# Moving one subtraction of the sliding-window attention from GpSimd to VectorE in a one-core trunk kernel

## The chip, the cores and the metric

The kernel runs on one core of one Trainium2 chip. The metric is the device time of one execution, in microseconds (us); less is better. A core has five engines that work at the same time, each through its own list of instructions in a fixed order: TensorE (PE in the profile, with its weight loads as PEld), VectorE (DVE), ScalarE (ACT), GpSimd (POOL) and SyncE (SP), which here only issues DMAs. An instruction that has to wait for another engine holds up everything behind it in its own list.

## The reference

One decoder layer is computed for a prompt of 2048 tokens (plus 16 meta tokens in front) and for a group of 8 x 4 sample tokens. Each token passes a normalisation, a wide input projection, three groups of heads side by side (HGRN2, mLSTM, and attention over a sliding window of 128 keys with a sink), an output projection and a SwiGLU feed-forward layer. The change touches the attention of the prompt, whose core is

```python
s = einsum('bnqhgd,bnshd->bnhgqs', q, k) * HD_C ** -0.5
s = where(mask, s, NEG_BIG)
mx = maximum(max(s, axis=-1), sink)
p = exp(s - mx)
den = sum(p, axis=-1) + exp(sink - mx)
o = einsum('bnhgqs,bnshd->bqnhgd', p / den, v)
```

There are 8 query heads in two groups (the variable `kv`) of four, 64 wide, and each block of 128 queries sees its own 128 keys and the 128 before them.

## The kernel before

The arithmetic is meant to be close to single precision, while TensorE is fed 16-bit operands. So an operand is split into a high part (rounded to float16) and a low part (the difference between the value and its high part, again in float16), and a product is made of three matmuls: high x high, high x low, low x high.

The prompt is worked through in tiles of 128 tokens. For each tile `project` makes the input projections in pieces of the weight matrix (named `qf`, `bqk`, `cq`, `ckv`, `aig` and `bvo`), all through the helper at L212, and then `mix` runs three generators side by side: `swa_prompt` (attention), `mlstm_prompt` and `hgrn_prompt`. After the mixer, from about 842 us on in the profiled execution, come the output projection, the preparation of the feed-forward operands and the feed-forward layer itself. One tile of the mixer takes about 46 us.

The order in which an engine's list is written is not the order of the source: the framework schedules the instructions with a timing model of its own when the program is built, so moving an instruction to another engine also changes the order of others around it. On the chip the lists are fixed, and engines wait for one another by semaphores.

In `swa_prompt` the steps for each tile are these. The scores of a head pair come from TensorE (L810) and are masked and reduced on VectorE (L813). ScalarE takes the exponentials and their sums (L819). VectorE makes the reciprocal of the denominators, `sden` (L824). Then, for each of the two groups `kv`:

- GpSimd multiplies the four heads' weights, 128 x 256 each, by the reciprocal (L834), in place in `pb`;
- ScalarE writes the high part `hi`, 128 x 1024, into the tile `ph` (L835);
- SyncE issues a DMA that transposes `hi` into `pT` (L836);
- GpSimd subtracts, `lo = pb - hi`, 128 x 1024, into the second half of `ph` (L837);
- SyncE issues the transposing DMA of `lo` (L838).

At the end TensorE multiplies the transposed weights with the values (L845, the tile `oc`), and ScalarE and VectorE write the result (L854, L855). `ph` has one buffer, so the high part of the second group (L835) can't be written before both transposes of the first group have read `ph`. `pT` has two buffers.

Beside it on VectorE run the HGRN2 levels (L540, L549, L551, each level feeding the next level's matmuls at L527), with their decay products `t` on GpSimd (L553); the mLSTM gates (L622 to L636, among them a series of tiny 128 x 4 instructions at L634), its row statistics (L648 to L676, which feed the matmul at L678) and its masked scores (L689, L698); and the low parts of the projections (L325, L350, L353), which wait for the high parts from ScalarE and are waited for by DMAs at L326 and L351.

Of the kernel before, what the change touches and what calls it, by code (L numbers as in the profile page):

```python
# [14 lines left out]
ALU = mybir.AluOpType  # L15
# [44 lines left out]
def trunk(ctx, tc, I, O, groups):  # L60
    nc = tc.nc
    V, S, G, T = nc.vector, nc.scalar, nc.gpsimd, nc.tensor
# [15 lines left out]
    def pmt(name="m"):  # L78
        return pm.tile([P, 512], F32, tag="m", name=nm(name))
# [42 lines left out]
    def zt(tag, shape, dt=F32, bufs=1):  # L122
        return pz.tile(shape, dt, tag=tag, bufs=bufs, name=nm(tag))
# [365 lines left out]
    def small(tag, cols=8):  # L489
        return am_(tag, [P, cols], bufs=2)  # L490
# [300 lines left out]
    def swa_prompt(s, yT, off):  # L791
        L = s.L
        prev = carry["kv"]
        blocks = ([prev] if prev else []) + [(s.kx, s.cvx)]
        nbk = len(blocks)
        W = nbk * P
        mask = (swm if s.chunk >= 2 else swm1).rearrange("p a k -> p (a k)")[:L, 2 * P - W :]
        mx = small("mx", 8)[:L]
        den = small("sden", 8)[:L]
        pms = []  # L800
        for kv in range(2):
            pb = zt(f"pb{kv}", [P, 4, 2 * P])
            pms.append(pb)
            for gp in range(2):
                ps = pmt("ss")
                for u in range(2):
                    g = 2 * gp + u
                    for o, (kx, _) in enumerate(blocks):
                        for a in range(2):
                            T.matmul(ps[:L, u * 256 + o * P : u * 256 + o * P + P], s.qx[kv][:, g], kx[:, kv, a], start=(a == 0), stop=(a == 1))  # L810
                for u in range(2):
                    hd = kv * 4 + 2 * gp + u
                    V.tensor_tensor_reduce(pb[:L, 2 * gp + u, :W], ps[:L, u * 256 : u * 256 + W], mask, 0.125 / (QS * QS), -3.0e38, ALU.add, ALU.max, mx[:, hd : hd + 1])  # L813
                yield
        ng = small("ng", 8)[:L]
        V.scalar_tensor_tensor(ng, mx, -1.0, nsink[:L], op0=ALU.mult, op1=ALU.min)
        for hd in range(8):
            pb = pms[hd // 4][:L, hd % 4, :W]
            S.activation(pb, pb, AF.Exp, bias=ng[:, hd : hd + 1], accum_out=den[:, hd : hd + 1])  # L819
        es = small("es", 8)[:L]  # L820
        V.tensor_tensor(es, ng, sink[:L], op=ALU.add)
        S.activation(es, es, AF.Exp)
        V.tensor_tensor(den, den, es, op=ALU.add)
        V.reciprocal(den, den)  # L824
        pts = []
        for kv in range(2):

            ph = zt("ph", [P, 2, 4, 2 * P], F16)
            pt = zt("pT", [P, 2, 8, P], F16, bufs=2)[:, :, : 4 * nbk, :L]
            pts.append(pt.rearrange("p a (g b) t -> p a b g t", b=nbk))  # L830
            hi, lo = (ph[:L, a].rearrange("p g k -> p (g k)")[:, : 4 * W] for a in range(2))
            pb = pms[kv][:L, :, :W]
            for g in range(4):
                G.tensor_scalar(pb[:, g], pb[:, g], den[:, kv * 4 + g : kv * 4 + g + 1], PS, op0=ALU.mult, op1=ALU.mult)  # L834
            S.activation(hi.rearrange("p (g k) -> p g k", g=4), pb, AF.Copy)  # L835
            nc.sync.dma_start(pt[:, 0], hi, transpose=True)  # L836
            G.tensor_tensor(lo.rearrange("p (g k) -> p g k", g=4), pb, hi.rearrange("p (g k) -> p g k", g=4), op=ALU.subtract)  # L837
            nc.sync.dma_start(pt[:, 1], lo, transpose=True)  # L838
            yield
        po = pmt("oc")  # L840
        order = [(b, p, r) for b in range(nbk) for p, r in ((0, 0), (1, 0), (0, 1))]
        for b, p, r in order:
            for kv in range(2):
                o_ = slice(kv * 64, kv * 64 + 64)
                T.matmul(po[o_, : 4 * L].rearrange("p (g t) -> p g t", g=4), blocks[b][1][:, p, o_], pts[kv][:, r, b], start=(b, p, r) == order[0], stop=(b, p, r) == order[-1])  # L845
        pv = po[:, : 4 * L].rearrange("p (g t) -> p g t", g=4)
        put_yT(yT, 4, pv, off, L, YS / (PS * VS))
        carry["kv"] = (s.kx, s.cvx)
        yield

    def put_yT(yT, j0, pv, off, L, scale=YS):
        hi = yT[:, 0, j0 : j0 + 4, off : off + L]
        lo = yT[:, 1, j0 : j0 + 4, off : off + L]
        S.activation(hi, pv, AF.Copy, scale=scale)  # L854
        V.scalar_tensor_tensor(lo, pv, scale, hi, op0=ALU.mult, op1=ALU.subtract)  # L855

    def mixer_prompt(s, yT, off):
        y = zt("y", [P, 512])
        interleave(swa_prompt(s, yT, off), mlstm_prompt(s, y[:, 256:512]), hgrn_prompt(s, y[:, 0:256]))
        finish_y(y, yT, off, s.L)  # L860
# [348 lines left out]
    with (  # L1209
# [136 lines left out]
        for gi, grp in enumerate(groups):  # L1346
# [35 lines left out]
            for rw in sum(rows2, []):  # L1382
# [9 lines left out]
                if t == 0:  # L1392
                    k = min(L, NS - r0)
# [313 lines left out]
```

## Time and profile before

| what | before |
|---|---|
| median of 3 runs | 2424.07 us (2414.37 to 2427.03) |
| the profiled execution | 2414.44 us |
| span of its instructions | 2412.7 us |
| busy: TensorE / VectorE / ScalarE / GpSimd | 92% / 70% / 39% / 50% of the span |
| mean granted TensorE clock | 0.970 |
| L837 on GpSimd | 34 instructions, the first at 91.7 us and the last at 837.9 us |

The last row says where the change acts: in the first 842 us, which hold all the mixer tiles of the prompt. The page's list of the chain that ended last names only the final additions and stores, a few us in all, so it says nothing about this stage; the stage has to be read from its windows, its waits and its order of time. In the rows that follow, "a <- b" behind an instruction is the tile that it writes and those that it reads, and a bracket at the end tells how long the engine was idle before the instruction and what ended that.

### The profile page before, as it was taken

Reading aid. Unit: us, or ns where it says so; the run is one execution under the profiler, and the core shown is the slowest. Engines: PE = TensorE matmul, PEld = TensorE weight load, DVE = VectorE, ACT = ScalarE, POOL = GpSimd, SP = SyncE. Lnnn points to the kernel's source line nnn. Section 1 sums busy time; section 2 is a strip of 40 time slices with the busy share of each in tenths; the row PEclk is TensorE's granted clock in tenths of the full one; section 3 lists DMA queues with packets and bytes.
Section 4 is the critical chain, followed back from the end, with each engine's and each line's share of the span. In section 5 each row is a group of like instructions: output and inputs, shape, how many; then the busy total and the mean of one; then the engine's idle time right before and its main releaser. Section 6 shows DMA issues by size and latency. Waiting matters only on the chain. (4 is left out here: it accounts for less than half of the span.)

```text
span 2412.7 us, 51978 instructions
## 1 busy us (share of the span) xinstructions
PE 2220.3 (92%) x20298; PEld 1607.4 (67%) x20298; DVE 1679.2 (70%) x4030; ACT 943.5 (39%) x2526; POOL 1211.7 (50%) x1629
## 2 busy tenths in 40 slices
PE   6989999999999899896989979889999999999996
PEld 6677767767776445444657556567686767888886
DVE  8788988988988756558879677746454535655546
ACT  7554455554554432334343434422212123332323
POOL 7344344444443464549778788744232324544435
PEclk9999999999999899997999989899999999999998
DMA  7232333333223755996436545684324247744441
GB/s 258 50 63 69 66 67 68 75 61 74 66 64 73 173 183 192 275 330 222 153 139 231 196 158 191 191 287 185 148 108 168 108 152 199 269 176 175 177 174 38
DMA packets 294329, 364.95 MB, mean 151 GB/s; under 512 B 203808, under 2 KB 234480, under 8 KB 294067
## 3 DMA queue, kind: packets, MB, share of 16 engines
q1 hardware_dynamic: 285090, 331.02, 43.6%
q0 software_dynamic: 4384, 15.93, 1.7%
q10 hardware_dynamic: 4608, 14.68, 1.7%
q8 instruction: 159, 2.61, 0.4%
q14 instruction: 88, 0.71, 0.1%
HBM read 212.24 MB, written 103.50 MB: 131 GB/s over the span
## 5 line engine op out<-in xcount | busy, mean ns | idle before, releaser
L1239 PE MATMUL s<-x,w 128*128 128x384 f16 (+1 forms) x5544 | 826.4, 312 | 14.8 <-DMA w<-wgu_scratch 6.2
L1239 PEld LDWEIGHTS <-w 128*128 128x128 f16 x5544 | 542.6, 98 | 296.5 <-issue 13.8
L1292 PE MATMUL dn<-w,hh 128*128 128x256 f16 (+1 forms) x4158 | 444.4, 278 | 56.0 <-ACT hh L1268 23.6
L1292 PEld LDWEIGHTS <-hh 128*128 128x128 f16 (+1 forms) x4158 | 379.6, 99 | 119.8 <-ACT hh L1268 27.8
L212 PEld LDWEIGHTS <-xT 128*128 128x128 f16 (+1 forms) x1992 | 177.4, 99 | 191.4 <-issue 25.2
L1268 ACT ACTIVATE hh<-tmp 128x384 f16<-128x384 f32 (+1 forms) x231 | 112.4, 494 | 280.4 <-DVE tmp L1262 164.5
L1248 POOL TENSOR_TENSOR tmp<-tmp,tmp 128x384 f32<-128x384 f32 (+1 forms) x66 | 65.3, 990 | 279.0 <-ACT tmp L1247 271.8
L1269 DVE TENSOR_TENSOR hh<-tmp,hh 128x384 f16<-128x384 f32 (+1 forms) x231 | 144.5, 633 | 74.2 <-ACT hh L1268 72.5
L212 PE MATMUL wo<-wo,xT 128*128 128x512 f16 x768 | 180.8, 394 | 9.5 <-DVE xn L992 4.6
L156 DVE SCALAR_TENSOR_TENSOR w<-raw,w 128x512 f16<-128x512 f32 (+1 forms) x136 | 111.9, 855 | 7.0 <-ACT w L155 6.9
L1250 DVE TENSOR_TENSOR tmp<-s,tmp 128x384 f32<-128x384 f32 (+1 forms) x66 | 34.2, 518 | 107.3 <-PE s L1239 107.3
L212 PE MATMUL d<-xT,qf 128*128 128x128 f16 (+1 forms) x1632 | 107.7, 220 | 0.0
L156 DVE SCALAR_TENSOR_TENSOR w<-sums,w 128x1024 f16<-128x1024 f32 x68 | 96.9, 1427 | 11.4 <-ACT w L155 11.4
L1259 ACT ACTIVATE tmp<-tmp 128x384 f32<-128x384 f32 (+1 forms) x132 | 61.6, 489 | 107.9 <-DVE tmp L1250 52.6
L212 PE MATMUL d<-xT,bqk 128*128 128x128 f16 (+1 forms) x1632 | 100.6, 221 | 3.2 <-DVE e L278 3.2
L1324 DVE SCALAR_TENSOR_TENSOR xr<-dn,xr 128x256 f32<-128x256 f32 x192 | 78.7, 417 | 34.4 <-PE dn L1292 30.2
L212 PEld LDWEIGHTS <-qf 128*128 128x128 f16 x1632 | 94.4, 100 | 9.1 <-issue 4.1
L212 PEld LDWEIGHTS <-bqk 128*128 128x128 f16 x1632 | 94.0, 100 | 5.4 <-issue 4.5
L212 PE MATMUL d<-xT,cq 128*128 128x128 f16 (+1 forms) x1632 | 96.2, 217 | 0.0
L212 PE MATMUL d<-bvo,xT 128*128 128x512 f16 (+1 forms) x408 | 96.2, 380 | 0.0
L1262 DVE SCALAR_TENSOR_TENSOR tmp<-tmp,tmp 128x384 f32<-128x384 f32 (+1 forms) x132 | 71.9, 558 | 34.1 <-POOL tmp L1249 32.6
L212 PE MATMUL d<-aig,xT 128*128 128x512 f16 (+1 forms) x408 | 92.4, 379 | 3.4 <-DVE g L358 3.4
(536 smaller groups left out, 4064.6 us busy)
## 6 DMA issues: line engine op xcount, KB each, us to landing
w<-wgu_scratch SPq DMA_DIRECT2D x88, 896.0 KB
wgu_scratch<-w SPq DMA_DIRECT2D x44, 896.0 KB
w<-wdn_scratch SPq DMA_DIRECT2D x44, 896.0 KB
raw<-in_w_ffn_in_dram SPq DMA_DIRECT2D x88, 256.0 KB
wdn_scratch<-w SPq DMA_DIRECT2D x22, 896.0 KB
xs<-in_x_prompt_dram SPq DMA_DIRECT2D x26, 512.0 KB
x_scratch<-pT ACTq DMA_DIRECT2D x28, 448.0 KB
raw<-in_w_ffn_out_dram SPq DMA_DIRECT2D x22, 512.0 KB
```

The costliest lines, as they stand in the source:

```text
L156: V.scalar_tensor_tensor(lo, src, scale, hi, op0=ALU.mult, op1=ALU.subtract)
L212: T.matmul(out, lh(k, a), rh(k, b), start=(n == 0), stop=(n == 3 * nk - 1))
L1239: T.matmul(out, A[k // 2][p][:, a, k % 2 * P : k % 2 * P + P], x2[r][:, k // 2, op, k % 2, :n], start=i == 0, stop=i == 11)
L1248: G.tensor_tensor(r12, r12, r22, op=ALU.add)
L1250: V.tensor_tensor(r11, prod(A12, B21), r11, op=ALU.add)
L1259: S.activation(d, d, AF.Silu, scale=UF)
L1262: V.scalar_tensor_tensor(d, v, UF * HS, d, op0=ALU.mult, op1=ALU.mult)
L1268: S.activation(hi, v, AF.Copy)
L1269: V.tensor_tensor(lo, v, hi, op=ALU.subtract)
L1292: T.matmul(out, hh[p][:, q, a, off : off + L], ws[q][r][:, b], start=(q, p, r) == order[0], stop=(q, p, r) == order[-1])
L1324: V.scalar_tensor_tensor(x[:L, cc], m, UD, x[:L, cc], op0=ALU.mult, op1=ALU.add)
```

## The change

One word of one line: the subtraction that makes the low part of the attention weights is issued on VectorE (`V`) and no longer on GpSimd (`G`). Operands, shapes, types and buffers stay as they are.

```diff
             S.activation(hi.rearrange("p (g k) -> p g k", g=4), pb, AF.Copy)
             nc.sync.dma_start(pt[:, 0], hi, transpose=True)
-            G.tensor_tensor(lo.rearrange("p (g k) -> p g k", g=4), pb, hi.rearrange("p (g k) -> p g k", g=4), op=ALU.subtract)
+            V.tensor_tensor(lo.rearrange("p (g k) -> p g k", g=4), pb, hi.rearrange("p (g k) -> p g k", g=4), op=ALU.subtract)
             nc.sync.dma_start(pt[:, 1], lo, transpose=True)
```

Thirty-four instructions move, two for each of the 17 mixer tiles (32 of 128 x 1024, two of 16 x 512 for the meta tokens). Since the scheduler runs again, other instructions move with them: up to about the middle of the program on the engines' lists the order differs, and the feed-forward layer behind it is in the same order as before.

GpSimd's list in one middle tile, as a difference (`-` stands in the kernel before only). `ph_8520` and `ph_8558` are the first and the second group's `ph`, `t_...` are the decay products of the HGRN2 levels.

```order
 L834 TENSOR_SCALAR pb_1047_8427<-pb_1047_8427,sden_8355 128x256 x4
 L553 TENSOR_TENSOR t_1077_8584<-t_1072_8556 128x8
-L837 TENSOR_TENSOR ph_8520<-pb_1036_8356,ph_8520 128x1024
 L553 TENSOR_TENSOR t_1082_8619<-t_1077_8584 128x2x2
 L373 TENSOR_TENSOR ga_9150<-ga_9150,gA_448 128x256
-L837 TENSOR_TENSOR ph_8558<-pb_1047_8427,ph_8558 128x1024
 L553 TENSOR_TENSOR t_1087_8639<-t_1082_8619 128x2
```

Both subtractions leave the list; the four multiplications of the second group (the first row shown) stand ahead of them before and after.

VectorE's list in the same tile, at the place where they come in.

```order
+L837 TENSOR_TENSOR ph_8520<-pb_1036_8356,ph_8520 128x1024
+L350 SCALAR_TENSOR_TENSOR kx_9109<-d_9060,kx_9109 64x128
 L540 COPY_PREDICATED att_8377<-lv_45_381,lv_8574 64x4x2x16 x2
 L549 TENSOR_TENSOR qz_465<-qz_465,t_1072_8556 64x2x4x16 x2
 L551 TENSOR_TENSOR k_8017<-k_8017,t_1072_8556 128x8x16
-L325 SCALAR_TENSOR_TENSOR qlo_9053<-d_8954,qx_1123_9052 64x512
-L350 SCALAR_TENSOR_TENSOR kx_9109<-d_9060,kx_9109 64x128 x2
+L350 SCALAR_TENSOR_TENSOR kx_9109<-d_9060,kx_9109 64x128
 L353 SCALAR_TENSOR_TENSOR cvx_9110<-d_9060,cvx_9110 128x128
 L358 SCALAR_TENSOR_TENSOR g_9119<-d_9060,gbias_454 128x8
 L622 SCALAR_TENSOR_TENSOR ax_9269<-g_9119 128x4
+L837 TENSOR_TENSOR ph_8558<-pb_1047_8427,ph_8558 128x1024
```

The two subtractions stand ten instructions apart in the new list, and one HGRN2 level and the low parts of the keys and values lie between them. Of the first fifteen full tiles this is the one with the least work between the two; in the sixteenth and last only four small copies stand between them.

SyncE's list in the same tile, which holds the DMAs of `ph`.

```order
+L326 DMA qx_1122_9051<-qlo_9053 64x512
 L836 DMA_TRANSPOSE pT_8521<-ph_8520 128x8x128
-L326 DMA qx_1122_9051<-qlo_9053 64x512
 L326 DMA qx_1123_9052<-qlo_9053 64x512
+L838 DMA_TRANSPOSE pT_8521<-ph_8520 128x8x128
 L351 DMA kx_9109<-kx_9109 64x256 x2
-L838 DMA_TRANSPOSE pT_8521<-ph_8520 128x8x128
 L836 DMA_TRANSPOSE pT_8559<-ph_8558 128x8x128
```

The transpose of the first low part (L838 of `pT_8521`) now stands ahead of the two copies of the keys (L351) and no longer behind them.

## The prediction

> **What bounds the kernel now.** I read the windows first, cut where the mixer tiles begin and end. Columns: length, then busy time and (x) instructions of PE, PEld, DVE, ACT and POOL, the granted clock, and the DMA share and rate.
>
> ```profile
> 0.00:120.00 120.00, 99.76 (x1362) 77.91 (x1363) 96.49 (x329) 74.52 (x211) 65.55 (x109) 0.97 0.48 154
> 120.00:842.00 722.00, 664.98 (x8009) 509.26 (x8006) 624.74 (x1985) 362.24 (x1206) 306.16 (x545) 0.99 0.34 77
> 842.00:2412.70 1570.70, 1455.52 (x10932) 1020.21 (x10932) 957.97 (x1717) 506.75 (x1111) 839.94 (x976) 0.96 0.53 185
> ```
>
> The subtraction lies in the first two rows. In the second TensorE is busy 665.0 of 722 us (92%) and VectorE 624.7 (87%); GpSimd, which gives the work up, is at 42%. So TensorE leaves 57.0 us idle there, and this is all that any edit of the other engines can win in that stage. Next I read what TensorE waits for (total us, times, longest):
>
> ```profile
> PE lv L527 <- DVE k L551: 24.6, 21, 3.8
> PE Mb L678 <- DVE mb L676: 20.4, 12, 4.7
> PE oc L845 <- DMA pT<-ph: 6.4, 8, 1.6
> ```
>
> 45 of the 57 us are waits for VectorE (HGRN2 levels, mLSTM row statistics). Only 6.4 us are waits for the transposed weights that the subtraction helps to make. So VectorE is second in line, and work added to it can surface on TensorE; GpSimd stands in none of these rows.
>
> **What goes away.** The costliest group of GpSimd in this stage:
>
> ```profile
> L837 POOL TENSOR_TENSOR ph<-pb,ph 128x1024 f16<-128x1024 f32 x32 | 68.9, 2154 | 25.0 <-ACT ph L835 25.0
> ```
>
> With two small ones this is 71 us of GpSimd time, which by itself is worth nothing, since nobody on TensorE waits for GpSimd. But the order of time shows a second cost. Start, duration, instruction; the first and the last of 23 cases, one in between, and the next tiny VectorE instruction behind that one:
>
> ```profile
> 134.56 2.16 POOL L837 TENSOR_TENSOR ph<-pb,ph 128x1024 f16<-128x1024 f32 x1 [3.29 <-ACT ph L835]
> 134.76 2.11 DVE L549 TENSOR_TENSOR qz<-qz,t 64x128 f32<-64x128 f32 x1
> 545.91 2.13 POOL L837 TENSOR_TENSOR ph<-pb,ph 128x1024 f16<-128x1024 f32 x1 [0.83 <-ACT ph L835]
> 545.95 2.12 DVE L634 SCALAR_TENSOR_TENSOR pp<-pp,z 128x4 f32<-128x4 f32 x1
> 548.32 0.15 DVE L635 SCALAR_TENSOR_TENSOR pp<-pp,z 128x4 f32<-128x4 f32 x1
> 837.85 2.20 POOL L837 TENSOR_TENSOR ph<-pb,ph 128x1024 f16<-128x1024 f32 x1 [4.38 <-ACT ph L835]
> 837.79 2.41 DVE L549 TENSOR_TENSOR qz<-qz,t 64x128 f32<-64x128 f32 x2
> ```
>
> A 128 x 4 instruction that takes 0.15 us takes 2.12 us when it meets the subtraction: VectorE stands still until GpSimd is done, although the profile counts it as busy. Taking from each VectorE instruction that overlaps an L837 the usual time of its own kind (the tenth percentile), 23 of the 34 subtractions stretch one by more than 0.1 us, together **39.7 us**. So the true cost of the subtraction to VectorE is already 39.7 us.
>
> **What is added.** No row has this subtraction on VectorE. The nearest rows (count, then minimum/median/maximum in ns) are one of the same width and types with one more operand, and one of the same operation and types with 384 elements:
>
> ```profile
> L205 DVE SCALAR_TENSOR_TENSOR xn<-xs,ss,xn x15: 1270/1280/1286, 34.3 to 655.2; 128x1024 f16<-128x1024 f32 x15
> L1269 DVE TENSOR_TENSOR hh<-tmp,hh x231: 432/551/1348, 1087.7 to 2368.0; 128x384 f16<-128x384 f32 x77, 128x280 f16<-128x280 f32 x39
> ```
>
> I take the first, 1.28 us: 32 x 1.28 = 41.0, and 1.3 for the two small ones: **42.3 us**. The low end scales the second up at one element per ns: 0.55 + 0.64 = 1.19 us, or 39.4 in all. The Trainium skill, "GPSIMD Engine Reference", section "Performance versus the Vector engine", gives a two-input elementwise operation as 1.96 times slower on GpSimd; by that factor the 2.15 us of the row above would be an estimated 1.10 us, the term 36 us and the result 2 us lower. Against the stretch that goes, the busy time of VectorE changes by 42.3 - 39.7 = +2.6 us: next to nothing.
>
> **A new wait.** The subtraction of the second group needs its high part, and that needs `ph` free of the first group's transposes. On GpSimd this wait harmed nobody; on VectorE everything behind it waits too (in the changed order the mLSTM gates and scores and the next HGRN2 level). The chain in one tile: first subtraction, its DMA on SyncE, second high part.
>
> ```profile
> 538.90 2.12 POOL L837 TENSOR_TENSOR ph<-pb,ph 128x1024 f16<-128x1024 f32 x1
> 541.55 1.31 SPq L838 DMA_TRANSPOSE pT<-ph  x1
> 544.78 1.06 ACT L835 ACTIVATE ph<-pb 128x1024 f16<-128x1024 f32 x1 [1.95 <-DMA pT<-ph]
> ```
>
> From the issue of the DMA to the high part are 3.23 us, then 1.06 us of writing it: 4.3 us at least from the end of the first subtraction to the start of the second, 4.9 with the 0.5 us that the DMA stood behind other issues here. What VectorE has to do meanwhile is in the changed order; its durations, for the tile with the least:
>
> ```profile
> 539.43 0.28 DVE L350 SCALAR_TENSOR_TENSOR kx<-d,kx 64x128 f16<-64x128 f32 x1
> 540.05 0.29 DVE L350 SCALAR_TENSOR_TENSOR kx<-d,kx 64x128 f16<-64x128 f32 x1 [0.34 <-ACT kx L349]
> 540.69 0.29 DVE L353 SCALAR_TENSOR_TENSOR cvx<-d,cvx 128x128 f16<-128x128 f32 x1 [0.34 <-ACT cvx L352]
> 540.90 0.15 DVE L358 SCALAR_TENSOR_TENSOR g<-d,gbias 128x8 f32<-128x8 f32 x1
> 541.09 0.16 DVE L622 SCALAR_TENSOR_TENSOR ax<-g 128x4 f32<-128x4 f32 x1
> 542.02 0.60 DVE L540 COPY_PREDICATED att<-lv,lv 64x128 f32<-64x128 int32 x2
> 542.66 0.59 DVE L549 TENSOR_TENSOR qz<-qz,t 64x128 f32<-64x128 f32 x2
> 543.26 0.29 DVE L551 TENSOR_TENSOR k<-k,t 128x128 f32<-128x128 f32 x1
> ```
>
> These add up to 2.65 us, with some 0.7 of waits for ScalarE (brackets). Done in the same way for all 16 full tiles the work between is 0.9 (the last tile) to 6.8 us, 4.1 on average. Against 4.3 us, with those waits counted as cover, VectorE would stand 5 us in all; against 4.9 and without them 15. I take **10 us**. The first subtraction waits for less:
>
> ```profile
> 534.65 0.20 DVE L824 RECIPROCAL sden<-sden 128x8 f32<-128x8 f32 x1
> 536.93 1.06 ACT L835 ACTIVATE ph<-pb 128x1024 f16<-128x1024 f32 x1 [0.16 <-POOL pb L834]
> ```
>
> That is 3.3 us from the reciprocal to the high part, and mostly over 3.6 us of VectorE work lie there in the changed order: nothing, in the first tiles up to 1 us each, within the bounds above.
>
> **A collision that stays.** The first subtraction will run while GpSimd multiplies the second group's weights. What that does is seen a little earlier in the same tile, against the same pair undisturbed (0.59 us, above):
>
> ```profile
> 535.02 3.75 POOL L834 TENSOR_SCALAR pb<-pb,sden 128x256 f32<-128x256 f32 x8 [2.50 <-DVE sden L824]
> 536.16 0.87 DVE L549 TENSOR_TENSOR qz<-qz,t 64x128 f32<-64x128 f32 x2
> ```
>
> 0.28 us more. I take 0.25 for each of 16 tiles, **4 us**; the bounds are 0 and one whole multiplication, 3.75 / 8 = 0.47 each, 8 us. The Trainium skill, "SBUF — State Buffer", section "Who interferes with whom", has the rule: a VectorE instruction with two SBUF inputs and a GpSimd instruction that reads SBUF share a port, and the one that comes second is blocked for the whole of the other. By it the subtraction keeps colliding from its new place and may hold GpSimd for 1.28 us in turn; without it this term is 0 and the result 1 us lower. The trace agrees as to the block (2.12 us).
>
> **What reaches TensorE.** VectorE's sum is 2.6 + 10 + 4 = **+16.6 us**. What such a delay costs is read in windows of 3.65 us from the start of each L837, that is the subtraction and 1.5 us behind it; three of the 34, and their sum:
>
> ```profile
> 582.83:586.48 3.65, 3.65 (x18) 1.67 (x17) 3.48 (x7) 1.04 (x3) 2.33 (x3) 1.00 0.47 90
> 593.49:597.13 3.64, 2.15 (x18) 1.63 (x16) 0.85 (x2) 0.34 (x2) 2.27 (x2) 1.00 0.47 89
> 837.85:841.50 3.65, 3.65 (x20) 1.82 (x20) 3.11 (x5) 0.35 (x2) 2.40 (x2) 1.00 0.44 84
> sum 124.09, PE 111.31 PEld 71.65 DVE 101.08 ACT 30.76 POOL 83.75; mean PE 3.27 PEld 2.11 DVE 2.97 ACT 0.90 POOL 2.46
> ```
>
> TensorE is idle for 124.1 - 111.3 = 12.8 us in all of them, 10.3%, hardly more than the stage's 7.9%. In the first window it runs 18 long projection matmuls back to back while VectorE stands: the projections of the next tile (`aig`, `bvo`) are the cover. So 39.7 us of stalls come with at most 12.8 us of idle TensorE, a share of 0.32, and 16.6 us more would bring about **+5 us**. Against that, the low parts are ready sooner: the subtraction is 0.9 us shorter, and the first one need not stand behind the second group's multiplications. I take half of the 6.4 us of waits at L845: **-3 us**. Sum: +2 us on the profiled execution, 2414.4 to 2416.4. The median shown (2424.1) is 9.6 us above that execution, and a median is what will be measured: 2424.1 + 2 = **2426 us**.
>
> **The rivals.**
>
> 1. *Slower: VectorE waits for the second high part.* Mechanism: the second subtraction at the head of VectorE's list. For it: VectorE is 87% busy, 45 us of TensorE's waits name it, and in seven of the 16 tiles the changed order has less than 4 us of work between the two subtractions. Against it: the cover by projections. With the upper bounds (15 of waiting, 8 of collision, 2.6) it is 26 us, and if all of it shows, 2450. It decides from a share of 12 / 26 = 0.46, where I take 0.32. Chance 0.23.
> 2. *Faster: the stretch was the price.* The 12.8 us of idle beside the subtractions and the 6.4 us at L845 go, and the new work falls into the 97 us (722 - 625) in which VectorE is idle: -19 us, 2405. Against it: TensorE's idle time beside the subtractions is near that of the stage, so most of it has other reasons. The Trainium skill's "GPSIMD Engine Reference", section "Engine selection", would have elementwise work on VectorE and so point this way. Chance 0.17.
> 3. *The stall only changes its name.* VectorE stood 1.2 us on average for each subtraction (39.7 / 34) and now works 1.28 us; TensorE sees no difference, 2424. This lies within the forecast's band.
>
> **How the numbers follow.** A measurement of this kernel tells about 0.5% (12 us) from no change. Forecast with rival 3: 0.60, from 2412 to 2436. The range reaches halfway and more into both others: 2408 to 2446. Faster by over 0.5%: 0.17; within: 0.60; slower: 0.23.
>
> **What would show it.** Right: L837 on VectorE at 1.25 to 1.3 us, no 128 x 4 instruction of 2 us left near it, VectorE's busy time in the stage within 10 us of 625, GpSimd's down by some 69, and idle time of VectorE "until ACT `ph` L835" of 5 to 15 us. TensorE's idle time in the stage stays near 57 us. Wrong: the subtraction takes 2 us on VectorE too (a collision in most cases, some 25 us more), or that idle time is over 25 us, or the new order of TensorE's list, which I can't price from this trace, alone moves the stage by more than 10 us.

## The result, and the profile after

| | before | after |
|---|---|---|
| median | 2421.63 us (6 runs, 2414.37 to 2427.92) | 2404.07 us (6 runs, 2400.87 to 2408.52) |
| the profiled execution | 2414.44 us | 2401.93 us |
| span | 2412.7 us | 2399.9 us |

The ratio is **0.9932, 95% interval 0.9913 to 0.9952**: the change makes the kernel some 16 us faster. The prediction of 2426 us, and the lower end of its range (2408), were missed. The second rival had named 2405.

Where the time came from is read from the windows between the same places of the two programs: from the first full tile's reciprocal (L824) to the fifteenth's, from there to the sixteenth's, to the last matmul of the output projection, and to the first product with `hh` in the feed-forward layer. First the kernel before (length, busy PE, PEld, DVE, ACT, POOL, granted clock, DMA):

```profile
123.20:765.40 642.20, 595.93 (x7532) 472.01 (x7529) 558.36 (x1778) 327.42 (x1104) 268.50 (x484) 0.99 0.31 67
765.40:827.10 61.70, 51.80 (x367) 28.45 (x365) 56.69 (x181) 29.36 (x88) 29.04 (x47) 0.92 0.69 167
827.10:1055.00 227.90, 201.56 (x1293) 104.06 (x1293) 126.83 (x235) 68.56 (x158) 113.15 (x161) 0.92 0.71 215
1055.00:1111.80 56.80, 55.34 (x338) 32.86 (x336) 44.66 (x52) 26.95 (x49) 45.59 (x49) 1.00 0.81 302
```

The same four stretches of the kernel after:

```profile
124.50:756.00 631.50, 594.52 (x7536) 471.19 (x7533) 553.98 (x1805) 325.35 (x1104) 215.74 (x456) 1.00 0.32 68
756.00:811.70 55.70, 48.74 (x338) 26.86 (x336) 52.15 (x167) 29.17 (x87) 21.00 (x42) 0.97 0.68 162
811.70:1034.00 222.30, 197.59 (x1313) 102.86 (x1313) 132.08 (x253) 69.06 (x159) 111.13 (x162) 0.95 0.72 220
1034.40:1098.90 64.50, 57.20 (x338) 33.58 (x337) 42.55 (x52) 27.22 (x49) 47.84 (x50) 0.95 0.86 290
```

The first fifteen tiles are 10.7 us shorter with nearly the same TensorE work (595.9 and 594.5 us busy), so TensorE's idle time there fell from 46.3 to 37.0 us. The last tile gives 6.0 more, of which 2.9 are idle time, and the stage with the output projection 5.6; in these two the granted clock was also higher (0.92 against 0.97 and 0.95), so that not all of it need come from the change. The start of the feed-forward layer gives 7.7 us back, at a clock of 0.95 against 1.00. Behind it both take 1301 us, and their order there is the same. The two profiled executions differ by 12.5 us and the medians by 17.6: the one before was among the fastest of its kernel, so some 5 us of the gain are not in these profiles.

What TensorE waits for in the mixer of the kernel after, and its subtraction on VectorE (minimum/median/maximum in ns, then what VectorE waited for in front of it):

```profile
PE lv L527 <- DVE k L551: 17.1, 19, 2.5
PE Mb L678 <- DVE mb L676: 16.3, 12, 3.1
PE oc L845 <- DMA pT<-ph: 6.4, 8, 1.7
...
L837 DVE TENSOR_TENSOR ph<-pb,ph x34: 673/1226/1405, 90.8 to 823.2; 128x1024 f16<-128x1024 f32 x32, 16x512 f16<-16x512 f32 x2
...
  ACT ph L835: 11.4, 13
```

The waits for the HGRN2 levels (L551) fell from 24.6 to 17.1 us and those for the mLSTM rows (L676) from 20.4 to 16.3. The wait for the transposed weights is 6.4 us as before. The subtraction takes 1.23 us, and VectorE waits 11.4 us for the high parts.

The order of time shows the stretch gone from the subtraction (stretch is the time by which VectorE's instructions are drawn out beside one of GpSimd) and still there beside another GpSimd instruction, the 128 x 256 product at L373:

```profile
538.90 0.73 POOL L373 TENSOR_TENSOR ga<-ga,gA 128x256 f32<-128x256 f32 x1 [0.27 <-DVE rr L626]
...
538.94 0.70 DVE L628 TENSOR_TENSOR z<-ax,rr 128x4 f32<-128x4 f32 x1
...
540.90 1.21 DVE L837 TENSOR_TENSOR ph<-pb,ph 128x1024 f16<-128x1024 f32 x1
542.03 0.35 DVE L634 SCALAR_TENSOR_TENSOR pp<-pp,z 128x4 f32<-128x4 f32 x2
```

Behind the subtraction two of the tiny instructions at L634 now take 0.35 us together, where one had taken 2.12. The second row set against the last tells the kinds apart: a 128 x 4 instruction of 0.70 us stands, one of some 0.17 works.

### The profile page after: what moved, and what is told of

Read it like the earlier page. It is cut to its first block, busy times and chain, and to the rows that moved or that the text cites. A ratio compares the mean times of both kernels' runs of the same rounds, so it can differ in the third digit from the quotient of the medians.

```text
span 2399.9 us, 51972 instructions
## 1 busy us (share of the span) xinstructions
PE 2215.4 (92%) x20298; PEld 1605.7 (67%) x20298; DVE 1673.4 (70%) x4064; ACT 941.8 (39%) x2526; POOL 1148.9 (48%) x1595
## 5 line engine op out<-in xcount | busy, mean ns | idle before, releaser
L1239 PE MATMUL s<-x,w 128*128 128x384 f16 (+1 forms) x5544 | 827.8, 312 | 20.4 <-DMA w<-wgu_scratch 7.8
L553 POOL TENSOR_TENSOR t<-t 128x8 f32<-128x8 f32 (+2 forms) x100 | 24.9, 249 | 188.2 <-DVE k L551 100.6
```

The source lines that it names most:

```text
L553: G.tensor_tensor(tn, tv[:, :, :, 0], tv[:, :, :, 1], op=ALU.mult)
L1239: T.matmul(out, A[k // 2][p][:, a, k % 2 * P : k % 2 * P + P], x2[r][:, k // 2, op, k % 2, :n], start=i == 0, stop=i == 11)
```

## The experiments

"Stretch" is counted throughout as in the prediction: over the VectorE instructions that overlap the GpSimd instruction in question, the time above the tenth percentile of their own kind. Before has 39.7 us of it. All ratios are to the kernel before on the same chip. Three theories were on trial: A, the gain is that VectorE no longer stands still behind GpSimd's subtraction; B, the gain is the other order that the scheduler wrote; C, the gain is that the low parts are ready sooner.

### A dead subtraction on GpSimd beside the new one

```diff
             V.tensor_tensor(lo..., pb, hi..., op=ALU.subtract)
+            G.tensor_tensor(pb, pb, hi.rearrange("p (g k) -> p g k", g=4), op=ALU.subtract)
```

> The changed kernel, and behind each subtraction on VectorE a second one of the same size on GpSimd, written in place into pb, whose result nobody reads (the next tile overwrites it). Theory A (standing VectorE): the gain came from GpSimd's subtraction no longer making a VectorE instruction of the HGRN2 levels or the gates stand still. Then the standing comes back, 25 to 40 us of stretched VectorE instructions, TensorE's waits for L551 rise again by 5 us or more, and the time is at least 10 us over the changed kernel's 2404: 2414 to 2430, ratio to before 0.997 to 1.004. Theory B (list order): the gain is the scheduler's other order; the time then depends on the new order alone and has no reason to move by the stretch. Theory C (low parts sooner): the low parts and their DMAs are as early as in the changed kernel, so the time stays at 2400 to 2408, ratio 0.993.

Measured: 2429.27 us, ratio 1.0040 (1.0025 to 1.0055). The dead instruction is L838 here; the trace shows it doing to VectorE what the old one did, and TensorE's first wait is up again:

```profile
555.03 2.13 POOL L838 TENSOR_TENSOR pb<-pb,ph 128x1024 f32<-128x1024 f32 x1 [2.23 <-DVE ph L837]
...
555.21 1.97 DVE L634 SCALAR_TENSOR_TENSOR pp<-pp,z 128x4 f32<-128x4 f32 x1
...
PE lv L527 <- DVE k L551: 21.0, 20, 2.8
```

The stretch is 40.8 us. The wait for L551 rose by 3.9 us, a little less than the 5 expected; another 6.3 (0.7 in the changed kernel) are waits for the gates at L634. With a GpSimd instruction that hardly anybody waits for (ScalarE once, 0.2 us) the kernel takes 26 us more (1.0040 - 0.9932, of 2421). That speaks for A and against C: TensorE waits 7.0 us for the transposed weights, where it waited 6.4. Two limits remain. The scheduler wrote other lists here too, so that this run alone doesn't rule out B. And of the 27 us between the two profiles 18 had come up by the sixteenth tile's reciprocal (829.5 against 811.7 us); the other 9 came behind it, where only two of the 34 dead subtractions run, so not all of the 26 us need be the standing.

### A dead fill in its place

```diff
             V.tensor_tensor(lo..., pb, hi..., op=ALU.subtract)
+            G.memset(pb, 0.0)
```

> The control for the dead GpSimd subtraction: the changed kernel, and behind each subtraction on VectorE a GpSimd instruction that fills pb with zeros (nobody reads it). It waits for the same and writes the same 128 x 1024 float32 values as the dead subtraction, but reads nothing. Theory A (standing because GpSimd reads): no stretch beside it, ratio to before 0.992 to 0.996, some 20 us below the dead subtraction's 2429. If GpSimd's extra instruction or the later release of pb was what cost there: ratio 1.000 to 1.004.

Measured: 2404.71 us, ratio 0.9932 (0.9912 to 0.9952), that of the changed kernel. The fill waits for the same subtraction and writes the same tile, but reads nothing: the stretch beside it is 2.0 us. Its lists are those of the changed kernel with the fills put in, and so not those of the dead subtraction. In the profile, two kinds of instruction with two inputs while a fill runs:

```profile
541.68 0.95 POOL L838 MEMSET pb<- 128x1024 f32 x1 [2.55 <-DVE ph L837]
...
541.81 0.58 DVE L549 TENSOR_TENSOR qz<-qz,t 64x128 f32<-64x128 f32 x2
542.41 0.29 DVE L551 TENSOR_TENSOR k<-k,t 128x128 f32<-128x128 f32 x1
```

One instruction of the kind at L549 took 2.11 us beside the old subtraction; here two take 0.58 together. The fill is shorter (0.95 us against 2.13), so the two differ in length as well; but a fill that stopped VectorE would still show as up to 0.9 us each, some 30 us, and it doesn't. So what makes VectorE stand is that GpSimd *reads* SBUF beside a VectorE instruction with two inputs there, not that it is busy. The Trainium skill, "SBUF — State Buffer", section "Who interferes with whom", says the same: VectorE instructions with two inputs in SBUF contend with GpSimd instructions that read SBUF and not with those that only write it. The traces agree on both halves (40.8 us of stretch beside 34 reading instructions, 2.0 us beside 34 fills).

### Only the second group, only the first group

```diff
-            V.tensor_tensor(lo..., pb, hi..., op=ALU.subtract)
+            eng = V if kv else G
+            eng.tensor_tensor(lo..., pb, hi..., op=ALU.subtract)
```

and with `G if kv else V`.

> Only the second group's subtraction is on VectorE, the first stays on GpSimd. In the profile of before the second ones carry about 27 of the 39.7 us of stretched VectorE time, the first ones 13. Theory A: about two thirds of the gain of 16 us, ratio 0.994 to 0.997, 8 to 15 us of stretch left beside L837 on GpSimd. Theory B: nothing says which way. Theory C: the last transposes decide when the product L845 can run and they follow the second subtraction: nearly all of the gain, ratio 0.993.

> Only the first group's subtraction is on VectorE, the second stays on GpSimd, so that VectorE never waits for the second high part (11.1 us in the changed kernel). Theory A: a third of the gain, ratio 0.997 to 0.999, 20 to 30 us of stretch left. Theory C: little, ratio 0.998 to 1.000, though the second high part can start sooner. If the ratio is at or below 0.993, the 11 us of waiting cost as much as the stretch that stays.

Measured: only the second 0.9968 (0.9950 to 0.9987), stretch left 12.4 us; only the first 0.9978 (0.9960 to 0.9995), stretch left 28.0 us. The two gains, 0.32% and 0.22%, add up to 0.54% of the 0.68% of both, and their order is that of the stretch that each takes away. This fits A. C, which gave the second nearly all and the first almost nothing, fits worse. The intervals overlap, so the shares are not exact, and these kernels have orders of their own as well.

With only the first moved, what the remaining subtraction hits can be seen: in 13 of 16 cases an instruction of the mLSTM gates (L622 to L636), never a level instruction (L549, L551), on which 25.8 of the 39.7 us fell in the kernel before. One of them, four merged instructions that take some 0.6 us undisturbed:

```profile
541.72 2.13 POOL L838 TENSOR_TENSOR ph<-pb,ph 128x1024 f16<-128x1024 f32 x1 [1.21 <-ACT ph L835]
...
541.78 2.68 DVE L634 SCALAR_TENSOR_TENSOR pp<-pp,z 128x4 f32<-128x4 f32 x4
```

In that profile the first fifteen tiles take 630.1 us, as in the changed kernel, although 28 us of stretch remain. It suggests that it matters which chain stands. But the whole time is some 10 us above the changed kernel's, so this stays a suggestion.

### No subtraction at all

```diff
-            G.tensor_tensor(lo..., pb, hi..., op=ALU.subtract)
-            nc.sync.dma_start(pt[:, 1], lo, transpose=True)
+            nc.sync.dma_start(pt[:, 1], hi, transpose=True)
```

> The subtraction is left out altogether: the second transposing DMA reads the high part again, so the low part of the attention weights is missing from the result. VectorE neither stands for it nor does it. Theory A: the stretch is gone as in the changed kernel, and 40 us of VectorE work and 11 us of waiting beside; since the work was placed under projection matmuls it is worth little: ratio 0.987 to 0.993, TensorE's idle time in the mixer stage 30 to 40 us. Theory B: anything. If the ratio is 0.985 or less, VectorE's plain work still costs in the changed kernel.

Measured: 2395.20 us, ratio 0.9902 (0.9884 to 0.9921), as A expected. TensorE's idle time in the first fifteen tiles is 36.4 us. This sets a scale: on GpSimd the subtraction costs 0.98% of 2421, 24 us; on VectorE 0.30%, 7 us. The interval overlaps that of the changed kernel, so the 7 us are not clear of nothing, and the second transposing DMA no longer waits for a low part either, so more is left out here than VectorE's work.

### A fill on GpSimd in place of the old subtraction

```diff
-            G.tensor_tensor(lo..., pb, hi..., op=ALU.subtract)
+            G.memset(lo, 0.0)
```

> The kernel before, with GpSimd filling the low part with zeros in place of the subtraction (the low part of the attention weights is left out): GpSimd still writes the same tile but reads nothing. Theory A (VectorE stands because GpSimd reads SBUF at the same time): no VectorE instruction is stretched beside it, ratio as without the subtraction, 0.988 to 0.993. If writing alone stops VectorE as well, 15 us of stretch or more show beside the fill and the ratio is above 0.994. Theory B (list order): nothing says which way.

Measured: 2407.71 us, ratio 0.9960 (0.9944 to 0.9977). Half a hit: the stretch is gone (1.6 us), but the gain is 10 us where at least 17 were expected. The profiled execution, 2401.7 us, lies at the lower end of the runs (2401.68 to 2417.64), and its mixer is as short as the changed kernel's (632.1 us for fifteen tiles), so it can't show where the rest is lost. This stays open, and it counts against 24 us as the price of the standing alone: here the standing is gone, VectorE gets no work for it, and 10 us are won.

### The subtraction at high priority

The subtraction under a block of high priority, once on GpSimd (before) and once on VectorE (after). It was meant to make the scheduler write other lists for the same work.

```diff
-            G.tensor_tensor(lo..., pb, hi..., op=ALU.subtract)
+            with tc.high_priority():
+                G.tensor_tensor(lo..., pb, hi..., op=ALU.subtract)
```

> The kernel before, with the subtraction on GpSimd issued at high priority, which makes the scheduler write another order and changes no work. Theory A: the stretch stays at 30 to 45 us; where it falls on HGRN2 levels (L549, L551) decides, so the ratio is 0.997 to 1.003 unless the new order moves it all to the gates. Theory B: the order alone is worth 10 us or more, so the ratio leaves 0.997 to 1.003 with the stretch on the levels unchanged at 20 to 30 us.

> The changed kernel, with the subtraction on VectorE issued at high priority: another order, the same work. Theory A: still no stretch by the subtraction, ratio to before 0.990 to 0.996. Theory B: as likely near 1.000 as near 0.993.

Measured: 0.9995 (0.9980 to 1.0011) with 36.1 us of stretch, of which 22.5 on the levels; and 0.9934 (0.9910 to 0.9958). Each is where its engine puts it. But the lists did not change: in the traces the instructions of each engine, and the DMAs, come in the order of the kernel before and of the changed kernel, to the last one. So these two runs say nothing about B; they are the same two kernels once more, and show how far two profiles of one order lie apart.

What B is worth must be read from the other runs, whose lists do differ from one another. TensorE's idle time in the first fifteen tiles (length of the window less busy PE), with the stretch that is left:

| order of the lists | kernel | stretch, us | TensorE idle, us |
|---|---|---|---|
| first | before; the same at high priority | 39.7; 36.1 | 46.3; 49.9 |
| second | dead subtraction | 40.8 | 50.2 |
| third | changed; the same at high priority; with the dead fill | 0; 0; 2.0 | 37.0; 37.4; 38.2 |
| fourth | no subtraction | 0 | 36.4 |
| fifth | fill in place of the old subtraction | 1.6 | 39.8 |
| sixth | only the second group | 12.4 | 39.1 |
| seventh | only the first group | 28.0, none on the levels | 37.7 |

The two orders with all of the stretch have 46 to 50 us, the three without it 36 to 40, though these three differ from one another as well. So in the stage where the subtraction runs the time goes with the standing and not with one lucky order. No pair holds the order fixed and takes the standing away, and behind the mixer, where these profiles differ by several us too, B stays open. The last row fits the suggestion above: stretch that misses the levels hardly shows on TensorE in this stage.

### The subtraction twice on VectorE

```diff
             V.tensor_tensor(lo..., pb, hi..., op=ALU.subtract)
+            V.tensor_tensor(lo..., pb, hi..., op=ALU.subtract)
```

> The changed kernel with the subtraction made twice on VectorE, one behind the other, with the same result: 41 us of VectorE work more, which the scheduler knows of and places, against the 39.7 us of standing that it doesn't know of. If work that is planned is cheaper than standing (theory A as it now stands): 3 to 10 us over the changed kernel, ratio to before 0.994 to 0.998. If a us of VectorE is a us of VectorE, planned or not: the whole gain goes, ratio 0.999 to 1.005. The kernel with the reciprocal folded in, which gave VectorE 16 us of work more and came out at 1.000, speaks for the second.

Measured: 2436.48 us, ratio 1.0067 (1.0048 to 1.0086): a miss for both. Its waits (TensorE's, then VectorE's) suggest that it isn't a plain price of VectorE work:

```profile
PE oc L846 <- DMA pT<-ph: 24.0, 18, 2.5
...
DVE kb L781 <- PE cu L779: 35.1, 14, 2.5
DVE qz L503 <- PE oa L590: 29.8, 14, 3.8
```

TensorE now waits 24.0 us for the transposed weights at L845 (L846 here) where it waited 6.4, and VectorE waits 65 us for TensorE at two places that cost it 6 in the changed kernel. That points to a second cliff, with the changed kernel ahead of it: where the subtraction ends later than the transposes need it, it is no longer covered. But this kernel's order is another one too, and one run doesn't tell the two apart.

### Two attempts at something better

The reciprocal folded into the writing of both parts, so that GpSimd does nothing in this attention; and the multiplications moved to ScalarE.

```diff
+        V.tensor_scalar(den, den, PS, None, op0=ALU.mult)
...
             for g in range(4):
-                G.tensor_scalar(pb[:, g], pb[:, g], den[:, ...], PS, op0=ALU.mult, op1=ALU.mult)
-            S.activation(hi..., pb, AF.Copy)
+                S.activation(hv[:, g], pb[:, g], AF.Copy, scale=den[:, ...])
             nc.sync.dma_start(pt[:, 0], hi, transpose=True)
-            V.tensor_tensor(lo..., pb, hi..., op=ALU.subtract)
+            for g in range(4):
+                V.scalar_tensor_tensor(lv_[:, g], pb[:, g], den[:, ...], hv[:, g], op0=ALU.mult, op1=ALU.subtract)
```

> Meant to beat both. The four multiplications on GpSimd (L834) go as well: ScalarE writes the high part of each head with the reciprocal as its scale, and VectorE makes the low part of each head as pb times reciprocal minus high part, four instructions of 128 x 256. GpSimd loses 60 us and the 8 us of stretch by L834; VectorE works some 1.7 us per group where it worked 1.23 (16 us more), ScalarE 16 us more; the high part comes some 1.5 us sooner. Theory A: what VectorE adds lies where the subtraction was, under projection matmuls, and the wait for the second high part shrinks: ratio to before 0.986 to 0.993. If VectorE's plain work counts after all: 0.995 to 1.000.

```diff
+        V.tensor_scalar(den, den, PS, None, op0=ALU.mult)
...
             for g in range(4):
-                G.tensor_scalar(pb[:, g], pb[:, g], den[:, ...], PS, op0=ALU.mult, op1=ALU.mult)
+                S.activation(pb[:, g], pb[:, g], AF.Copy, scale=den[:, ...])
```

> Meant to beat the changed kernel: the four multiplications per group (L834) move from GpSimd to ScalarE, as four copies with the reciprocal as scale; one tiny VectorE instruction per tile is added. GpSimd then does nothing in this attention and the 8.4 us of VectorE stretched by L834 go, at the price that the dead subtraction showed (27 us of time for 40 of stretch): some 5 us, ratio to before 0.989 to 0.993. Against it: ScalarE gets some 64 us of work in the mixer stage, where it is busy half of the time, and its list stands in order too; if the projections' high parts or the exponentials wait behind the copies, TensorE's waits rise and the ratio is 0.995 or more.

Measured: 1.0000 (0.9984 to 1.0015) and 1.0155 (1.0131 to 1.0179). Neither beats the changed kernel, though neither has any stretch by L834 left. The fold came out where its expectation put it if VectorE's plain work counts after all: 16 us of work more, and the whole gain gone. With the fold VectorE works 55.9 us on the low parts in place of 39 and TensorE waits longer for the transposes:

```profile
L839 DVE SCALAR_TENSOR_TENSOR ph<-pb,sden,ph 128x256 f16<-128x256 f32 x126 | 55.9, 484 | 10.3 <-ACT ph L836 10.1
...
PE oc L847 <- DMA pT<-ph: 11.9, 7, 3.4
```

With the copies on ScalarE, VectorE waits for that engine's list, for the high parts of the weights and of the values of the next tile:

```profile
DVE ph L838 <- ACT ph L836: 36.1, 18, 4.1
DVE cvx L353 <- ACT cvx L352: 31.6, 9, 3.8
```

68 us of such waiting, where the changed kernel has 14.5, against 8 us of stretch saved. How much of the fold's loss is VectorE's work and how much the later transposes stays open.

## Why the prediction was wrong

- *What goes away.* Right, and the heart of the matter: 39.7 us of VectorE time stood behind GpSimd. The dead subtraction and the fills show that reading SBUF is what does it, and in the mixer tiles TensorE's idle time is 46 to 50 us with all of it and 36 to 40 without, whatever the order.
- *What is added.* Right: 40.9 us by the rows of the trace (34 instructions), predicted 42.3. The 36 us by the factor of 1.96 would have been too low: the medians, 2129 ns on GpSimd and 1226 on VectorE, are a factor of 1.74 apart.
- *The new wait.* Right: 11.4 us, predicted 10, and 10.2 of them for the second group.
- *The collision that stays.* Mis-sized: hardly any of the 4 us. The longest of the 34 subtractions takes 1.41 us against a median of 1.23. The multiplication at L834 waits instead (twice 2.11 us, median 0.48); ScalarE's wait for it rose from 8.3 to 10.0 us, and TensorE waits for it nowhere.
- *Low parts sooner, -3 us.* Wrong: the wait at L845 is 6.4 us before and after, and in several tiles its DMA still stands behind the copies of the keys on SyncE.
- *What reaches TensorE.* **This is the step that failed.** The prediction added standing, working and waiting of VectorE into one sum, +16.6 us, and passed it on with one share, 0.32. So the standing that goes and the work that comes cancelled out. The runs show two prices. Against the kernel without the subtraction, the 39.7 us of standing cost 24 us, a share of 0.6; the 40.9 us of work and 11.4 us of waiting that replace them cost 7 us together, a share of 0.14. By TensorE's idle time in the first fifteen tiles the two are 9.9 us (46.3 - 36.4) and 0.6 (37.0 - 36.4). So the share of the standing alone is not well known, between a quarter and 0.6, and 0.32 lies within; what was wrong is to charge the work and the wait that replace it at the same rate. Why they are so cheap is not shown. A likely reason is that the scheduler knows of the work and places it under cover, while it knows nothing of the standing, which falls on whatever runs: 25.8 of 39.7 us fell on the levels that TensorE waits for most. But it holds for these 41 us only: the kernels with 16 us more (the fold) and with 41 us more (the subtraction twice), planned as well, lost the whole gain.
- The 12.8 us were no bound either. They are TensorE's idle time during each subtraction and in the 1.5 us behind it, but a delayed level can be paid for later, at a next matmul of the same chain. The same windows in the kernel after still hold 7.5 us of idle time (124.09 - 116.58), a fall of 5.3, while in all of the sixteen tiles it fell by 12.2 (9.3 and 2.9): more than half of the fall lies outside the windows. That it stays under 12.8 is chance. The row:

```profile
sum 124.09, PE 116.58 PEld 67.56 DVE 110.02 ACT 32.91 POOL 22.28; mean PE 3.43 PEld 1.99 DVE 3.24 ACT 0.97 POOL 0.66
```

- *The rivals.* The second had the right mechanism and nearly the time, 2405. The nearness is luck: of the 19 us it was made of, the 6.4 at L845 did not go at all, and of the 12.8 beside the subtractions 5.3 did. It was put at 0.17 because TensorE's idle time beside the subtractions was hardly above the stage's average, the same narrow windows. The first, VectorE waiting for the second high part, came true as a wait (11.4 us) but not as a price that shows.
- The median before is 2421.6 over six runs where the three shown had 2424.1; that moves the forecast by 2 us and explains nothing.

## What to carry to other kernels

A busy VectorE in a profile may be a VectorE that stands: where a tiny two-input instruction takes as long as the GpSimd instruction beside it, that GpSimd instruction has a price in VectorE's time, and moving it to VectorE can pay although VectorE is the busier engine by far. Don't net such standing against work at one rate: here the work cost much less than the standing that it replaced. And look for the cost of a delay beyond the windows next to it. Moving still more work the same way did not pay here: the next microseconds on VectorE or ScalarE ran into waits of their own. And before a run is taken as a test of another order, the order in its trace has to be compared: a request to the scheduler may change nothing.

## What the runs showed of the hardware

GpSimd's fill of 128 x 1024 (0.95 us) leaves VectorE's instructions with two inputs in SBUF alone, and its subtraction of the same size (2.13 us) stops them: 2.0 against 40.8 us of stretch beside 34 instructions each. The kernels with the one and with the other are 26 us apart, though their lists differ too. Most of the little stretch that the fills leave falls on instructions with one input: in the kernel with the fill in place of the old subtraction a 128 x 4 instruction at L632, 0.17 us as a rule, took 0.99 us beside a fill of 0.95. When the collision is the other way round, GpSimd pays: two of its 128 x 256 multiplications, with the subtraction inside their span, take 2.11 us in the kernel after (median 0.48).
